# Moving the norms' small sums to VectorE, and giving the list scheduler a different clock, in an fp32 encoder kernel

## The chip, the cores and the metric

The kernel runs on one core of a Trainium2 chip, as one launch. The metric is the device time of that launch in microseconds. A core has a matrix engine (TensorE, PE in the profile, with its weight loads as PEld), VectorE (DVE), ScalarE (ACT), GpSimd (POOL) and SyncE (SP, which here only issues DMAs). Each engine works off its own instructions in the order in which they were written, and waits where an input isn't there.

## The reference

Two encoder layers on a sequence of 256 rows of 1024 numbers, in fp32. Each layer has a mixer and a feed-forward part:

```
h = rms_norm(x, n1);  proj = h @ w_in                # 1024 -> 2560
qa, ka, va, qd, kd, vd, qc, kc, vc = split(proj)     # heads of 64
q, k of each group: rms_norm per head, d and c with rotary positions
out_a = neighbourhood_attention(4 heads, bias rpb)   # 2-D window
out_d = dilated_window_attention(6 heads)            # 3 patterns merged
out_c = gqa_block_attention(6 heads, 2 kv heads)     # full
x = x + concat(rms_norm(out_a), rms_norm(out_d), rms_norm(out_c)) @ w_out
h = rms_norm(x, n2);  g, u = split(h @ w_gate_up)    # 2 x 2816
g = depthwise_conv(g, 3 taps) + b
x = x + (gelu(g) * u) @ w_down
```

## The kernel before

**Arithmetic.** Every matrix product is three matmuls on parts of 32-bit numbers: each factor is split into a high part (rounded by a copy) and a low part (the difference), and `mm3` adds high x high, high x low and low x high. Weights arrive by DMA as `wp_raw`; ACT casts `wp_hi`, DVE subtracts `wp_lo`. The same is done with activations: `act_hT` (the normed x, transposed), `act_ch` and `act_cl` (softmax results, transposed, and later the gated values), `act_mixT_hi` and `act_mixT_lo` (attention results). Results stand in PSUM tiles `psa_a` (512 columns) and `psw_w`.

**Stages of a layer.** x is transposed into hT; the projections are made in the order d0, d1, cq, akv, aqk; the three groups of heads follow in the order d, c, a. For a head: scores (half-height matmuls, `act_o` for d), softmax on DVE and ACT (`act_s2k`), transposes by a matmul with `const_ident`, then the weighing of values (`const_v`). The next projections, and then the out-projections of finished groups, are handed out between the heads, so that PE has work while the softmax runs. After the last out-projections x (`const_x`) is normed and transposed again and the feed-forward part begins.

**Norms of q and k.** `normed` squares a piece of the projection (for d0, d1 and cq on ACT with a running sum; for the others on ACT with a reduction on DVE: `small_ss`), calls `rstd_of` (`small_ms` = ss / 64 + eps, then `small_rstd` = ms to the power -1/2, always on POOL), and scales the piece into `act_z`. For d0 and d1 DVE scales the first half of the heads in one instruction and ACT the others one by one. `mean_squares` does the like for the norms of x (`small_ssx`, `small_s1x`, `small_mex`, `small_rx`); `small_he` is an eps derived from it. `group_rstd` sums squares of a finished attention group (`act_sqm`, added on POOL).

**Bias rows.** `na_repeat` copies 28 rows of 31 numbers 64 times beside each other on POOL (`act_nab` from `small_few`) and writes them to DRAM, from where `na_diagonals` reads them back skewed.

**Kept weights.** The last six out-projection units of the second layer are loaded and split during the first layer's feed-forward part, written to DRAM (`dram_khi`, `dram_klo`), and loaded again in the second layer's attention by DMAs that POOL issues (`wp_hi<-dram_khi` and so on; the last into tiles `act_kc` and `act_qc` of earlier stages).

**What sets the order.** The program is first recorded by `Plan`, 5,000-odd operations with their dependences. `Plan.order` is a list scheduler with a clock of its own: `cost` gives each operation a duration, `handover` the time from one engine's result to another's start, `LANDS` the assumed landing times of the first 13 DMAs, and two constants in `order` the start and landing of every later one. At each step it takes, over all engines, the operation that can start first; between equals the lower rank wins, which is the place in the program plus offsets, among them `PLACES`, a table from an operation's number to a shift. `emit` writes the instructions in that order, which is why nearly every row of the profile has one line, L496. Tiles come from pools of few buffers, and a load waits until its buffer's last reader is done.

Of the kernel before, what the change touches and what calls it, by code (L numbers as in the profile page):

```python
# [14 lines left out]
AF = mybir.ActivationFunctionType  # L15
# [3 lines left out]
P = 128  # L19
# [32 lines left out]
LANDS = (4100, 3300, 5300, 3450, 6000, 6900, 7700, 8800, 9700, 10600, 11500, 11550, 11600)  # L52
# [177 lines left out]
def handover(a, b):  # L230
    return HANDOVER.get((a, b), 52 if b == "PE" else 60)
# [321 lines left out]
def encoder_kernel(  # L553
# [400 lines left out]
    for l in range(DEPTH):  # L954
# [59 lines left out]
        me, rx = mean_squares(f"n1{l}")  # L1014

        he = small.tile([P, NT], F32, tag="he", name=f"he{l}", bufs=2)
        nc.gpsimd.tensor_scalar(he, me, EPS, None, ALU.mult)

        wv.until("d0")

# [619 lines left out]
```

## Time and profile before

| | us |
|---|---|
| three runs | 606.33, 606.69, 609.0 (median 606.69) |
| the profiled execution | 605.31 |
| its span | 603.5 |
| PE busy in it | 595.9 |
| DVE busy | 484.2 |
| ACT busy | 425.2 |
| POOL busy | 86.7 |

The span is the time from the first to the last instruction in the profile of one execution; the execution's own time is longer by what lies around it. The profile has views for the busy time of each engine, for groups of like instructions, for the waits of an engine (what ended its idle time), for the chain of work that ended last, and a timeline of single instructions.

### The profile page before, as it was taken

What the parts mean: (1) busy time and instruction counts of PE and PEld (TensorE: products, weight loads), DVE (VectorE), ACT (ScalarE), POOL (GpSimd) and SP (SyncE); (2) the same over time, 40 slices, a digit from 0 to 9 for tenths busy, and PEclk for the clock granted to TensorE, in tenths of its full rate; (3) what the DMA queues carried; (4) which work ended last, traced back from release to release, by engine and by line L of the source; (5) the groups of instructions that cost most, each with busy time, mean ns of one, the idle gap of its engine ahead of it and who ended that gap; (6) DMA issues with size and microseconds to landing.
All of it is one profiled execution on the core that took longest, in us unless ns stands there. A gap on an engine that the chain in (4) does not pass through costs nothing.

```text
span 603.5 us, 9483 instructions
## 1 busy us (share of the span) xinstructions
PE 595.9 (99%) x3304; PEld 505.3 (84%) x3304; DVE 484.2 (80%) x991; ACT 425.2 (70%) x1049; POOL 86.7 (14%) x130
## 2 busy tenths in 40 slices
PE   9999999999999999999999999999999999999997
PEld 6887888888888888888888787887888888888886
DVE  4799988989679898877968897858877777787766
ACT  7879899786666776656688897776765656556652
POOL 2761131105200000000021314412000000000000
PEclk9999999999999999999999999999999999999999
DMA  8992305355589899997655444932565556555501
GB/s 290 379 267 79 119 31 170 138 198 205 172 251 310 287 333 340 320 307 283 208 183 169 141 140 175 325 132 71 185 235 183 173 202 209 174 179 205 183 27 71
DMA packets 89503, 121.42 MB, mean 201 GB/s; under 512 B 10072, under 2 KB 72120, under 8 KB 89456
## 3 DMA queue, kind: packets, MB, share of 16 engines
q1 hardware_dynamic: 87184, 112.17, 55.6%
q0 software_dynamic: 1728, 8.39, 4.0%
q8 instruction: 26, 0.43, 0.3%
q10 hardware_dynamic: 544, 0.26, 0.1%
q14 instruction: 21, 0.17, 0.1%
HBM read 110.93 MB, written 9.88 MB: 200 GB/s over the span
## 4 chain that ended last, share of the span: by engine, by line
PE 77%; DVE 6%; POOL 5%; DMA 5%; issue 3%; ACT 3%; SPq 1%; DVEq 0%; POOLq 0%; ACTq 0%
PE psw_w L496 47%; PE psa_a L496 30%; POOL small_rstd L496 2%; ACT act_s2k L496 2%; DVE const_x L496 1%; DMA wp_hi<-dram_khi 1%; DMA wp_lo<-dram_klo 1%; SPq L496 1%; DVE wp_lo L496 1%; DVE act_z L496 1%; DMA const_x<-in_x_dram 1%; DMA small_few<-in_rpb_dram 1%; POOL small_ms L496 1%; DVE act_s2k L496 1%; ACT wp_hi L496 0%
## 5 line engine op out<-in xcount | busy, mean ns | idle before, releaser
L496 DVE TENSOR_TENSOR wp_lo<-wp_raw,wp_hi 128x512 fp32r<-128x512 f32 (+1 forms) x316 | 233.4, 767 | 43.6 <-ACT wp_hi L496 38.8
L496 ACT CAST wp_hi<-wp_raw 128x512 fp32r<-128x512 f32 (+1 forms) x316 | 201.7, 689 | 28.4 <-PE psw_w L496 21.2
L496 PE MATMUL psw_w<-act_hT,wp_hi 128*128 128x512 f32 x704 | 178.1, 393 | 0.4 <-DVE act_hT L496 0.4
L496 PEld LDWEIGHTS psw_w<-act_hT,wp_hi 128*128 128x128 f32 x704 | 128.6, 188 | 26.6 <-DVE act_hT L496 1.2
L496 PE MATMUL psa_a<-wp_hi,act_hT 128*128 128x512 f32 x320 | 104.1, 398 | 0.3 <-ACT act_hT L496 0.3
L496 PE MATMUL psw_w<-act_hT,wp_lo 128*128 128x256 f32 x704 | 96.4, 279 | 0.0
L496 PEld LDWEIGHTS psw_w<-act_hT,wp_lo 128*128 128x128 f32 x704 | 92.5, 188 | 4.2
L496 ACT COPY act_s2k<-psw_w 128x256 f32<-128x256 f32 x88 | 32.2, 372 | 57.0 <-PE psw_w L496 56.8
L496 PEld LDWEIGHTS psa_a<-wp_hi,act_hT 128*128 128x128 f32 x320 | 59.1, 188 | 12.3 <-ACT act_hT L496 0.5
L496 PE MATMUL psa_a<-wp_lo,act_ch 128*128 128x512 f32 (+1 forms) x176 | 67.8, 387 | 0.0
L496 PE MATMUL psa_a<-wp_hi,act_ch 128*128 128x512 f32 (+1 forms) x176 | 67.6, 388 | 0.0
L496 PE MATMUL psa_a<-wp_hi,act_cl 128*128 128x512 f32 (+1 forms) x176 | 64.8, 387 | 0.0
L496 PE MATMUL psa_a<-wp_lo,act_hT 128*128 128x512 f32 x160 | 62.8, 395 | 0.0
L496 DVE TENSOR_TENSOR act_s2k<-psw_w,act_s2k 128x256 f32<-128x256 f32 x88 | 36.5, 421 | 28.8 <-ACT act_s2k L496 28.5
L496 PEld LDWEIGHTS psa_a<-wp_hi,act_cl 128*128 128x128 f32 x176 | 33.0, 188 | 6.8
L496 PEld LDWEIGHTS psa_a<-wp_lo,act_ch 128*128 128x128 f32 x176 | 33.0, 188 | 6.8
L496 PEld LDWEIGHTS psa_a<-wp_hi,act_ch 128*128 128x128 f32 x176 | 32.9, 188 | 6.7
L496 DVE SCALAR_TENSOR_TENSOR act_s2k<-act_s2k,act_cw,act_s2k 128x255 f32<-128x255 f32 x88 | 36.8, 477 | 0.1
L496 PEld LDWEIGHTS psa_a<-wp_lo,act_hT 128*128 128x128 f32 x160 | 30.1, 188 | 6.1 <-DVE wp_lo L496 0.2
L496 POOL TENSOR_TENSOR small_rstd<-small_ms,const_mh 128x2 f32<-128x2 f32 (+3 forms) x26 | 32.3, 1242 | 14.1 <-DVE small_ms L496 12.5
L496 ACT ACTIVATE act_s2k<-act_s2k 128x512 f32<-128x512 f32 x22 | 13.9, 633 | 25.2 <-DVE act_s2k L496 25.2
L496 ACT ACTIVATE act_s2k<-act_s2k,small_rs 128x256 f32<-128x256 f32 x64 | 29.2, 511 | 0.8 <-DVE small_rs L496 0.7
(130 smaller groups left out, 800.1 us busy)
## 6 DMA issues: line engine op xcount, KB each, us to landing
wp_raw<-in_w_gate_up_dram SPq DMA_DIRECT2D x44, 1024.0 KB, 4.9
wp_raw<-in_w_down_dram SPq DMA_DIRECT2D x22, 1024.0 KB, 4.9
wp_raw<-in_w_in_dram SPq DMA_DIRECT2D x16, 512.0 KB, 5.6
wp_raw<-in_w_in_dram SPq DMA_DIRECT2D x8, 1024.0 KB, 6.6
wp_raw<-in_w_out_dram SPq DMA_DIRECT2D x8, 768.0 KB, 4.3
wp_raw<-in_w_in_dram SPq DMA_DIRECT2D x16, 256.0 KB, 3.6
dram_khi<-act_mixT_hi SPq DMA_DIRECT2D x4, 768.0 KB, 4.1
dram_klo<-act_mixT_lo SPq DMA_DIRECT2D x4, 768.0 KB, 10.0
```

What stands on the lines that cost most here:

```text
L496: getattr(o.engine.real, o.method)(*map(real, o.args), **{k: real(v) for k, v in o.kw.items()})
```

## The change

Four things, with no change to the mathematics and with the same matmuls:

1. `rstd_of` makes `small_ms` always on VectorE; `small_s1x`, `small_mex` and `small_he` go to VectorE too. The power stays on POOL. 30 small instructions move.
2. `na_repeat` copies in four instructions of 16 repetitions each.
3. `normed` lets one engine scale a whole piece: ACT the d1 pieces, head by head, DVE all others, d0 among them.
4. The scheduler's clock: earlier `LANDS`, 180 instead of 52 ns from any engine to PE, later start (POOL's DMAs) and landing (all DMAs) of transfers, and a new `PLACES` table.

```diff
-LANDS = (4100, 3300, 5300, 3450, 6000, 6900, 7700, 8800, 9700, 10600, 11500, 11550, 11600)
+LANDS = (4000, 3300, 4800, 3450, 5400, 6200, 7500, 7900, 8600, 9400, 9950, 10150, 10350)
...
 def handover(a, b):
-    return HANDOVER.get((a, b), 52 if b == "PE" else 60)
+    return HANDOVER.get((a, b), 180 if b == "PE" else 60)
 PLACES = {
-    69: 675, 174: 69, 175: 485, 176: 81, 201: 382, 299: 271, 372: 236, 390: 27, 400: 25, 409: 64, 508: 25, 568: 374,
...
+    51: 27, 63: -214, 81: 932, 98: 230, 130: -463, 139: 398, 155: 65, 169: 146, 175: 246, 176: 223, 183: -207,
...
                 ring = e if i < self.first_loads else "SP"
-                end = max(at + 1360, wires.get(ring, 0.0))
+                end = max(at + (2100 if e == "POOL" else 1360), wires.get(ring, 0.0))
...
-                end = wires[ring] + 1000
+                end = wires[ring] + 1600
                 if i < self.first_loads:
                     end = LANDS[sum(p.method == "dma_start" for p in ops[:i])]
...
         ms = small.tile([P, n], F32, tag="ms", name=f"ms_{name}")
-        by = nc.vector if width > HD else nc.gpsimd
-        by.tensor_scalar(ms, ss, 1.0 / width, eps, ALU.mult, ALU.add)
+        nc.vector.tensor_scalar(ms, ss, 1.0 / width, eps, ALU.mult, ALU.add)
...
-        nc.gpsimd.tensor_tensor(s1, ss[:, :, 0], ss[:, :, 1], op=ALU.add)
+        nc.vector.tensor_tensor(s1, ss[:, :, 0], ss[:, :, 1], op=ALU.add)
         me = small.tile([P, NT], F32, tag="mex", name=f"me_{name}", bufs=2)
-        nc.gpsimd.tensor_scalar(me, s1, 1.0 / D, EPS, ALU.mult, ALU.add)
+        nc.vector.tensor_scalar(me, s1, 1.0 / D, EPS, ALU.mult, ALU.add)
...
-        nc.gpsimd.tensor_copy(
-            rows_.rearrange("p (n c) -> p n c", c=RPB_C),
-            nabs["few"].unsqueeze(1).to_broadcast([NR, GRID_W, RPB_C]),
-        )
+        for i in range(0, GRID_W, 16):
+            nc.gpsimd.tensor_copy(
+                rows_.rearrange("p (n c) -> p n c", c=RPB_C)[:, i : i + 16],
+                nabs["few"].unsqueeze(1).to_broadcast([NR, 16, RPB_C]),
+            )
...
-        nc.gpsimd.tensor_scalar(he, me, EPS, None, ALU.mult)
+        nc.vector.tensor_scalar(he, me, EPS, None, ALU.mult)
...
-            n = nh // 2 if name[0] == "d" else nh
-            nc.vector.tensor_tensor(
-                z[:, :n],
-                ps[:, : n * HD].rearrange("p (h d) -> p h d", d=HD),
-                r[:, :n].unsqueeze(2).to_broadcast([P, n, HD]),
-                op=ALU.mult,
-            )
-            for h in range(n, nh):
-                nc.scalar.activation(z[:, h], ps[:, h * HD : (h + 1) * HD], AF.Copy, scale=r[:, h : h + 1])
+            if name[:2] == "d1":
+                for h in range(nh):
+                    nc.scalar.activation(z[:, h], ps[:, h * HD : (h + 1) * HD], AF.Copy, scale=r[:, h : h + 1])
+            else:
+                nc.vector.tensor_tensor(
+                    z[:, :nh],
+                    ps[:, :w].rearrange("p (h d) -> p h d", d=HD),
+                    r.unsqueeze(2).to_broadcast([P, nh, HD]),
+                    op=ALU.mult,
+                )
```

Since the scheduler's clock and table change, most instructions change places. Three of them follow; a tile's number at the end of its name is its buffer, and the numbers differ between the kernels.

**PE, first layer, ahead of the first softmax result.** `act_hT` with `wp_hi` or `wp_lo` is a projection matmul of 512 columns; the row with `const_ident` and `act_s2k` is the first transpose of a softmax result. Before, the rows from the last projection's start to it:

```order
L496 MATMUL psa_a_309<-wp_hi_142,act_hT_148 128x512
L496 MATMUL psa_a_309<-wp_lo_150,act_hT_148 128x512
L496 MATMUL psa_a_309<-wp_hi_142,act_hT_148 128x512 x2
L496 MATMUL psa_a_309<-wp_lo_150,act_hT_148 128x512
L496 MATMUL psa_a_309<-wp_hi_142,act_hT_148 128x512 x2
L496 MATMUL psa_a_309<-wp_lo_150,act_hT_148 128x512
L496 MATMUL psa_a_309<-wp_hi_142,act_hT_148 128x512 x2
L496 MATMUL psa_a_309<-wp_lo_150,act_hT_148 128x512
L496 MATMUL psa_a_309<-wp_hi_142,act_hT_148 128x512
L496 MATMUL psw_w_170<-const_ident_89,act_s2k_220 128x128
```

These are all the rows between the last scores and that transpose: 12 matmuls. After, the last rows ahead of it:

```order
L499 MATMUL psa_a_298<-wp_lo_146,act_hT_143 128x512
L499 MATMUL psa_a_292<-wp_hi_242,act_hT_143 128x512
L499 MATMUL psa_a_292<-wp_lo_251,act_hT_143 128x512
L499 MATMUL psa_a_292<-wp_hi_242,act_hT_143 128x512
L499 MATMUL psa_a_298<-wp_hi_137,act_hT_143 128x512 x2
L499 MATMUL psa_a_298<-wp_lo_146,act_hT_143 128x512
L499 MATMUL psa_a_298<-wp_hi_137,act_hT_143 128x512
L499 MATMUL psa_a_298<-wp_hi_242,act_hT_143 128x512
L499 MATMUL psa_a_298<-wp_lo_251,act_hT_143 128x512
L499 MATMUL psw_w_116<-const_ident_88,act_s2k_205 128x128 x4
```

There are 24 matmuls between the last scores and that transpose now (the ten shown and 14 ahead of them), and five more stand ahead of the scores.

**PE, first layer, from the second half of the out-projections to the feed-forward part.** `const_ident` with `const_x` transposes x, `act_hT` with `wp_hi` first in such a row is the feed-forward part. Before:

```order
L496 MATMUL psw_w_124<-const_ident_89,const_x_79 128x128
L496 MATMUL psw_w_83<-const_ident_89,const_x_79 128x128
L496 MATMUL psw_w_124<-const_ident_89,const_x_79 128x128 x3
L496 MATMUL psa_a_342<-wp_hi_142,act_mixT_lo_871 128x512
L496 MATMUL psw_w_83<-const_ident_89,const_x_79 128x128 x3
L496 MATMUL psa_a_160<-wp_hi_142,act_mixT_lo_871 128x512
L496 MATMUL psa_a_160<-wp_hi_142,act_mixT_hi_797 128x512
L496 MATMUL psa_a_160<-wp_lo_150,act_mixT_hi_797 128x512
L496 MATMUL psa_a_160<-wp_hi_142,act_mixT_lo_871 128x512
L496 MATMUL psw_w_117<-act_hT_148,wp_hi_244 128x512
```

After:

```order
L499 MATMUL psw_w_116<-const_ident_88,const_x_79 128x128
L499 MATMUL psw_w_123<-const_ident_88,const_x_79 128x128
L499 MATMUL psa_a_292<-wp_lo_146,act_mixT_hi_851 128x512
L499 MATMUL psa_a_292<-wp_hi_137,act_mixT_lo_862 128x512
L499 MATMUL psw_w_116<-const_ident_88,const_x_79 128x128 x3
L499 MATMUL psw_w_123<-const_ident_88,const_x_79 128x128 x3
L499 MATMUL psw_w_169<-act_hT_143,wp_hi_137 128x512
```

Of the five out-projection matmuls behind the first transposes of x two are left.

**POOL, second layer, the kept weights.** A DMA row loads a kept weight. Before:

```order
L496 TENSOR_TENSOR small_rstd_338<-small_ms_329,const_mh_85 128x2
L496 TENSOR_TENSOR act_sqm_918<-act_sqm_918,act_sqm_817 128x256
L496 DMA wp_hi_142<-dram_khi_2023 128x1536
L496 DMA wp_lo_255<-dram_klo_2053 128x1536
L496 TENSOR_SCALAR small_ms_356<-small_ss_410,small_he_3058 128x8
```

and the second load of `wp_hi_142`, further on:

```order
L496 TENSOR_TENSOR small_rstd_484<-small_ms_477,const_mh_85 128x2
L496 DMA act_kc_908<-dram_klo_2641 128x1024
L496 DMA act_kc_903<-dram_khi_2627 128x1024
L496 DMA act_qc_679<-dram_khi_2757 128x1024
L496 DMA wp_hi_142<-dram_khi_2340 128x1536
```

After:

```order
L499 TENSOR_TENSOR small_rstd_324<-small_ms_321,const_mh_83 128x2
L499 DMA wp_hi_137<-dram_khi_2028 128x1536
L499 DMA wp_lo_146<-dram_klo_2097 128x1536
L499 TENSOR_TENSOR act_sqm_917<-act_sqm_917,act_sqm_856 128x256
L499 DMA wp_lo_251<-dram_klo_2215 128x1536
```

and

```order
L499 TENSOR_TENSOR small_rstd_490<-small_ms_469,const_mh_83 128x2
L499 DMA act_kc_900<-dram_klo_2650 128x1024
L499 DMA wp_hi_137<-dram_khi_2345 128x1536
L499 DMA act_qc_709<-dram_khi_2738 128x1024
L499 DMA act_qc_720<-dram_klo_2763 128x1024
```

The first two loads have moved ahead of the sum of squares that they stood behind, and the second load of that `wp_hi` now stands behind one of the loads into `act_kc` and `act_qc` where it stood behind three.

33 rows, old and new, of the table PLACES are left out of this document.

## The prediction

> **What bounds the kernel now.** I read the page first: span, busy shares and chain.
>
> ```profile
> span 603.5 us, 9483 instructions
> PE 595.9 (99%) x3304; PEld 505.3 (84%) x3304; DVE 484.2 (80%) x991; ACT 425.2 (70%) x1049; POOL 86.7 (14%) x130
> PE 77%; DVE 6%; POOL 5%; DMA 5%; issue 3%; ACT 3%; SPq 1%; DVEq 0%; POOLq 0%; ACTq 0%
> ```
>
> TensorE (PE) carries the program: it is drawn busy for 99% of the span and holds 77% of the chain that ended last. The other 23% are places where the chain leaves it. The 99% flatters, because ends of matmuls are modelled; the pace is seen where the chain holds nothing else:
>
> ```profile
> 550.01 5.45 PE psa_a L496 x24
> 555.46 11.13 PE psw_w L496 x64
> ```
>
> 24 matmuls of 512 columns take 5.45 us, 227 ns each. The other row holds 32 of 512 and 32 of 256: (11.13 - 32 x 0.227) / 32 = 0.12 us for 256 columns. The change issues the same matmuls, so it can only remove what comes above this pace. Where that lies, the busy time by stretch tells (us of PE, PEld, DVE, ACT, POOL, then granted clock, DMA share, GB/s):
>
> ```profile
> 30.00:60.00 30.00, 29.55 (x163) 23.85 (x162) 28.39 (x84) 26.19 (x95) 11.86 (x20) 1.00 0.62 176
> 90.00:120.00 30.00, 29.81 (x188) 24.79 (x188) 27.09 (x66) 25.44 (x70) 4.43 (x5) 1.00 0.45 156
> 120.00:330.00 210.00, 210.00 (x1108) 180.24 (x1107) 173.50 (x305) 144.81 (x314) 19.09 (x29) 1.00 0.76 255
> 330.00:360.00 30.00, 29.93 (x177) 24.59 (x176) 27.17 (x90) 27.37 (x98) 8.38 (x12) 1.00 0.46 150
> 360.00:390.00 30.00, 29.23 (x192) 24.71 (x191) 23.57 (x56) 23.42 (x68) 12.16 (x18) 1.00 0.65 221
> 390.00:420.00 30.00, 28.90 (x182) 23.95 (x181) 22.38 (x57) 21.49 (x59) 6.88 (x10) 1.00 0.37 132
> ```
>
> The clock is full everywhere, and the first feed-forward part (120 to 330) shows no idle PE. PE waits only in the two attention parts, 30 to 120 and 330 to 420, where VectorE (DVE) is busy for 27 to 28 of 30 us. The timeline of PE gives the waits one by one (start, duration drawn, idle ahead and what ended it):
>
> ```profile
> 10.56 0.50 PE L496 MATMUL psa_a<-wp_hi,act_hT 128*128 128x512 f32 x1 [0.31 <-ACT act_hT L496]
> ...
> 47.25 0.39 PE L496 MATMUL psa_a<-wp_hi,act_hT 128*128 128x512 f32 x1
> 47.86 0.33 PE L496 MATMUL psw_w<-const_ident,act_s2k 128*128 128x128 f32 x1 [0.22 <-ACT act_s2k L496]
> ...
> 52.95 0.36 PE L496 MATMUL psw_w<-act_ch,const_v 128*128 128x256 f32 x1
> 53.43 0.39 PE L496 MATMUL psw_w<-act_cl,const_v 128*128 128x256 f32 x1
> ...
> 118.23 0.40 PE L496 MATMUL psa_a<-wp_hi,act_mixT_lo 128*128 128x512 f32 x1
> 118.82 0.50 PE L496 MATMUL psw_w<-act_hT,wp_hi 128*128 128x512 f32 x1 [0.19 <-DVE act_hT L496]
> ...
> 372.95 0.40 PE L496 MATMUL psa_a<-wp_hi,act_mixT_hi 128*128 128x512 f32 x1
> 374.11 0.50 PE L496 MATMUL psa_a<-wp_lo,act_mixT_hi 128*128 128x512 f32 x1 [0.77 <-DMA wp_lo<-dram_klo]
> ...
> 393.43 0.28 PE L496 MATMUL psw_w<-act_cl,const_v 128*128 128x256 f32 x1
> 394.31 0.50 PE L496 MATMUL psa_a<-wp_hi,act_mixT_hi 128*128 128x512 f32 x1 [0.60 <-DMA wp_hi<-dram_khi]
> ```
>
> A wait costs start to start less the pace. 47.25 to 47.86: 0.61 - 0.23 = 0.38. 52.95 to 53.43: 0.48 - 0.12 = 0.36. 118.23 to 118.82: 0.36. 372.95 to 374.11: 0.93. 393.43 to 394.31: 0.76. At 10.56 it is the 0.31 shown and about the 0.16 that the modelled ends hide elsewhere (0.38 - 0.22, 0.93 - 0.77). Sum 3.3 us. The idle PE of the windows quoted is 0.45 + 0.19 + 0.07 + 0.77 + 1.10 = 2.6 us, of which these rows' brackets after 30 us show 0.22 + 0.19 + 0.77 + 0.60 = 1.8. The rest, 0.8 us, is short waits with the hidden part that each brings (some 0.16 us); I estimate 2 us in all. So some 5.3 us of 603.5 are to be had.
>
> **The change, part by part.** The prices, as groups by form (count, busy us, mean ns of one, idle before, releaser):
>
> ```profile
> L496 POOL TENSOR_SCALAR small_ms<-small_ss,small_he 128x8 f32<-128x8 f32 x8 | 3.5, 438 | 23.4 <-DVE small_ss L496 13.9 <-ACT act_s2k L496 9.1
> L496 POOL TENSOR_TENSOR small_s1x<-small_ssx 128x2 f32<-128x2 f32 x4 | 1.4, 358 | 174.2 <-ACT act_s2k L496 174.2
> L496 DVE TENSOR_SCALAR small_ms<-small_ss 128x2 f32<-128x2 f32 x6 | 1.0, 164 | 0.1
> L496 DVE TENSOR_TENSOR act_z<-psa_a,small_rstd 128x512 f32<-128x512 f32 x4 | 2.7, 684 | 0.0
> L496 DVE TENSOR_TENSOR act_z<-psa_a,small_rstd 128x256 f32<-128x256 f32 x4 | 1.7, 425 | 4.5 <-ACT act_z L496 2.0 <-POOL small_rstd L496 1.7 <-issue 0.7
> L496 DVE TENSOR_TENSOR act_z<-psa_a,small_rstd 128x128 f32<-128x128 f32 x8 | 2.3, 289 | 1.7 <-POOL small_rstd L496 1.5 <-ACT act_z L496 0.2
> L496 ACT ACTIVATE act_z<-psa_a,small_rstd 128x64 f32<-128x64 f32 x24 | 5.9, 335 | 6.7 <-DVE act_z L496 4.6 <-POOL small_rstd L496 2.1
> L496 ACT ACTIVATE act_s2k<-psa_a 128x64 f32<-128x64 f32 x72 | 15.4, 255 | 2.3 <-PE psa_a L496 2.3
> ```
>
> Small sums: 30 operations leave GpSimd (POOL) for VectorE. One costs 0.44 us on POOL (128x8) and 0.164 us on DVE. DVE gets at most 30 x 0.164 = 4.9 us; the six ms that DVE does already show 0.1 us idle before them, so they cost no wait there. Each norm's chain, square, sum, power, scaling, gets about 0.27 us shorter. That pays only where the scaling is waited for: DVE's 1.7 + 1.5 us and ACT's 2.1 us idle behind small_rstd. None of it ends a PE wait quoted above directly, so the sum takes nothing for it, with 0 and +0.5 us as bounds.
>
> Scaling by one engine: per d0 piece (4 in all) DVE does 128x512 for 128x256 (+0.26 us) and ACT four 128x64 less; per d1 piece (4) DVE loses a 128x128 (-0.29) and ACT gets two 128x64. DVE: 4 x 0.26 - 4 x 0.29 = -0.1 us; ACT: 4 x (2 - 4) x 0.335 = -2.7 us. ACT is not full in the windows, so it is worth nothing by itself; bounds 0 and +0.3, since two idles of one half behind the other (2.0 and 4.6 us in the rows) end.
>
> Bias rows in four copies:
>
> ```profile
> 17.11 1.89 DVE L496 TENSOR_TENSOR wp_lo<-wp_raw,wp_hi 128x512 fp32r<-128x512 f32 x3
> 20.21 1.03 DVE L496 TENSOR_TENSOR wp_lo<-wp_raw,wp_hi 128x512 fp32r<-128x512 f32 x1 [1.21 <-ACT wp_hi L496]
> ...
> 18.71 1.99 POOL L496 COPY act_nab<-small_few 28x1984 f32<-28x1984 f32 x1 [2.98 <-DMA small_few<-in_rpb_dram]
> ```
>
> The copy keeps POOL for 1.99 us ahead of the first norm's sum. In the new order two quarters stand ahead of the first power, so the first norm gains about 1 us; PE has no wait between 10.56 and 47.25, so this too is cover, not time: 0. Four starts instead of one cost POOL a few tenths where it has idle time. The rows also show a subtraction of 1.03 us, begun while the copy ran, against 1.89 / 3 = 0.63 before.
>
> The Trainium skill, SBUF — State Buffer, section Who interferes with whom, says that a VectorE instruction with two SBUF inputs and a GpSimd instruction that reads SBUF exclude each other for a whole instruction. The 0.40 us of stretch agree. By it the quarters would hold DVE for at most 0.5 us at a time, and the gain of at most 0.4 us a layer would fall where PE doesn't wait: the sum stays.
>
> Planner's clock and places: this moves nearly everything, and here the time is made. Place by place, in the new order:
>
> - Start, wait of 0.47 at 10.56 for ACT's part of hT. Casts of weights stand in other places, and DVE's hT is waited for earlier. I take +0.3 (bounds -0.2 and +0.47).
> - First heads of the first layer. Ahead of the first transpose of a softmax result stand 17 more 512-wide matmuls (12 of them between scores and transpose: 24, not 12), 3.9 us of PE work, against some 0.7 us more on ACT. The 0.38 at 47.86 should go. Ahead of the first weighing of values PE has 3.9 us more too, but DVE four more wp_lo (4 x 0.63) and nine small sums (9 x 0.07 to 9 x 0.164, by the spacing below): 3.1 to 4.0 us. So of the 0.36 at 53.43, and of about 0.3 of short waits ahead of it, I take half to go. Together +0.85 (bounds 0 and +1.0).
> - End of the first attention. Between the last value matmul and the feed-forward part stand three matmuls less, between the last transposes of the first half of x and that part two instead of five. The chain that PE waits for there is no shorter. -0.7 = 3 x 0.23 on top of the 0.36 (bounds -0.7 and 0).
> - Reloads of kept weights in the second layer, next.
>
> ```profile
> 113.75 0.16 DVE L496 TENSOR_SCALAR small_ms<-small_ss 128x2 f32<-128x2 f32 x1
> 113.82 1.28 DVE L496 TENSOR_TENSOR wp_lo<-wp_raw,wp_hi 128x512 fp32r<-128x512 f32 x2
> ...
> 363.69 1.10 POOL L496 TENSOR_TENSOR act_sqm<-act_sqm,act_sqm 128x256 f32<-128x256 f32 x1 [4.97 <-ACT act_sqm L496]
> 364.74 0.80 POOL L496 DMA_DIRECT2D wp_hi<-dram_khi  x1
> ...
> 385.28 0.56 POOL L496 DMA_DIRECT2D wp_hi<-dram_khi  x1
> ...
> 365.52 8.54 DMA wp_lo<-dram_klo
> ...
> 385.28 8.98 DMA wp_hi<-dram_khi
> ```
>
> (The first two rows give the spacing of a small sum on DVE: 0.07 us.) The first reload stands in POOL's queue behind a sum that waited 4.97 us for ACT; the load of wp_lo then takes 8.54 us, and PE waits 0.93 for it. In the new order both loads come ahead of that sum and are held by their buffer alone; by my count of the matmuls between the buffer's last use and the need they have about 10 us of PE's work for 9.3 us of issue and transfer. The wait of 0.93 goes, barely. The load at 385.28 was issued behind three others of about its own 0.56 us and now stands behind one: 1.1 us earlier, against 0.76 of wait. I take +1.6 of 1.69; bounds 0 (the transfers share the queue differently) and +1.69.
>
> For this size, 768 KB, the Trainium skill (DMA: Bandwidth & Descriptors, section Anatomy of one DMA — SWDGE (gpsimd) path) gives 2.0 us plus bytes / 436e3, an estimate of 3.8 us. By it no reload would be waited for, and the 1.6 us would not be there to win; the trace has 8.54 and 8.98 and decides.
>
> - The short waits, 2 us by the estimate above: the new clock assumes 180 ns, not 52, from an engine's result to PE, which puts results further ahead wherever another matmul can be taken. I take 1.0 (bounds 0 and 2.0).
> - DVE's load: +4.9 - 0.1 us in parts of the program where it has 1.6 to 2.9 us idle per 30. I take -0.25 (bounds -3 and 0).
>
> Sum: 0.3 + 0.85 - 0.7 + 1.6 + 1.0 - 0.25 = 2.8 us gained. Against the profiled execution of 605.31 us that is 602.5. The median of the runs, 606.69, lies 1.38 above that execution, so the forecast is 603.9.
>
> **The rivals.**
> *All waits go.* The slack of 180 ns removes the waits named and the short ones, and none comes in their place: -5.3 us, 601.4. For it: the feed-forward part, planned by the same code, has none. Against it: the end of the first attention has less cover than before.
> *Given back.* VectorE is the bound of the attention parts: of its 4.9 us about half (2.3) comes back on PE, in front of transposes and value matmuls: -2.8 + 2.3 = -0.5, 606.2. For it: 28.39 and 27.17 of 30 us busy; against it: the spacing of 0.07, with which 30 sums are 2.1 us.
> *Slower.* A small sum waits in VectorE's queue for ACT's squares, as POOL did (9.1 us idle behind ACT for the 128x8 alone), and the wp_lo and softmax work behind it waits too. Twelve sums (d0, d1 and cq pieces, six a layer) depend on ACT's squares. If each stands one us too early, DVE loses 6 us a layer, of which its idle time in 30 to 60 and 330 to 360 hides 1.61 and 2.83: 7.6 us later, less 2.8 gained: 611.5. It decides from about 0.6 us each (2.0 + 0.8 = 2.8). Against it: POOL is off PE's path and its idle time tells nothing of the order on DVE, where the planner places a sum by its own estimate of the squares' end (row of 255 ns each).
> *Doesn't do what it says.* LANDS and start moves change only the first 12 us; the reloads' waits stay. It gains 0.3 to 1 us: 606.
>
> **How the numbers follow.** A change of 0.5%, 3.03 us (0.005 x 606.69), is about what a measurement here tells from none; that bound, 603.66, lies next to my forecast. Forecast 0.45, own range 602 to 605.4, of which 0.19 falls beyond the bound and 0.26 within. All waits go 0.22 (faster). Given back 0.17 and does nothing 0.05 (same). Slower 0.11. So faster 0.41, same 0.48, slower 0.11. The range runs from 600.6 (601.4 less 0.8, the rest of short waits if my estimate of 2 is low) to 607.3 (given back, and the end of the first attention one us worse); outside it lie slower, 0.11, and some 0.07 below.
>
> **What would show it.** Right: no idle marked DMA on PE around 372 and 393, none at 47 and 53 us; a wait of about 1 us for hT, not 0.36, where the first feed-forward part begins; DVE some 3 to 5 us busier, ACT 2.7 us and POOL about 10 us less; the same number of matmuls. Wrong: idle of DVE ahead of small_ms released by ACT; a reload landing over 10 us after its issue; PE idle for act_cl or act_hT in new places in 30 to 120 us. If the time is the same although those waits are gone, the end of the attention parts took it back.

## The result, and the profile after

The changed kernel takes 602.26 us (median of 4 runs, 602.02 to 602.48), the kernel before 607.07 us beside it (4 runs, 606.33 to 609.0). The ratio is 0.9916 with a 95% interval of 0.9892 to 0.994: 4.8 us less. Measured again later it was 602.78 against 607.93 us, ratio 0.991 (0.9887 to 0.9934). The forecast of 603.9 us lay 1.6 us too high, and the time fell within its range; of the cases, it lies between the forecast and "all waits go" (601.4), nearer to the latter. The profiled execution took 602.47 us, 2.84 less than that of before; where the other 2 us come from is part of what follows.

Part of it is TensorE's granted clock, which the profiler gives for each run: of the 51 runs of the kernel before that stand beside the experiments, the 27 with a mean granted clock of 0.999 or 1.000 took 605.1 to 608.4 us (median 606.7) and the 24 with 0.994 to 0.998 took 607.9 to 611.4 (median 609.1), while all of the changed kernel's ten runs had 0.999 or 1.000 (median 602.5); at the full clock the change is worth some 4.3 us.

The page of the changed kernel, busy shares and chain:

```profile
span 600.7 us, 9486 instructions
PE 594.5 (99%) x3304; PEld 506.0 (84%) x3304; DVE 487.8 (81%) x1017; ACT 424.2 (71%) x1041; POOL 74.7 (12%) x106
PE 95%; DVE 2%; ACT 1%; DMA 1%; issue 1%; POOL 0%; SPq 0%; POOLq 0%
```

The busy shares hardly tell a difference. The chain does: PE holds 95% of it where it held 77%, and GpSimd and the reloads have left it. The same stretches as before:

```profile
30.00:60.00 30.00, 30.00 (x166) 24.86 (x165) 28.98 (x86) 27.33 (x105) 9.18 (x15) 1.00 0.66 206
90.00:120.00 30.00, 28.86 (x181) 23.89 (x180) 27.30 (x67) 25.83 (x71) 4.20 (x5) 1.00 0.47 160
330.00:360.00 30.00, 30.00 (x173) 24.54 (x171) 25.36 (x85) 26.55 (x91) 5.10 (x5) 1.00 0.33 107
360.00:390.00 30.00, 30.00 (x215) 25.68 (x215) 24.73 (x63) 24.02 (x70) 12.20 (x16) 1.00 0.71 239
390.00:420.00 30.00, 30.00 (x187) 26.09 (x184) 23.83 (x62) 22.79 (x63) 5.23 (x7) 1.00 0.51 180
```

In both attention parts PE is drawn busy throughout, but for 90 to 120, where it is idle for 1.14 us against 0.19 before. The view of PE's waits (us in total, times, longest) names what is left:

```profile
PE psw_w L499 <- DVE act_hT L499: 1.1, 1, 1.1
PE psw_w L499 <- POOL const_mh L499: 1.0, 1, 1.0
PE psa_a L499 <- ACT act_hT L499: 0.3, 1, 0.3
```

The second is the start of the program, which both kernels have. The first is the wait ahead of the first feed-forward part; the third, at 7.57 us, is for ScalarE's part of hT, as the wait at 10.56 was before. In PE's timeline the waits at 47 and 53 us are gone. At the first reload two matmuls stand at the pace, where there was a wait of 0.93 us, and at the feed-forward part there is a gap:

```profile
373.08 0.40 PE L499 MATMUL psa_a<-wp_hi,act_mixT_hi 128*128 128x512 f32 x1
373.31 0.40 PE L499 MATMUL psa_a<-wp_lo,act_mixT_hi 128*128 128x512 f32 x1
...
117.00 0.82 PE L499 MATMUL psw_w<-const_ident,const_x 128*128 128x128 f32 x6
118.87 0.50 PE L499 MATMUL psw_w<-act_hT,wp_hi 128*128 128x512 f32 x1 [1.06 <-DVE act_hT L499]
```

I summed for each stretch what PE's matmuls take above the pace (start to start, less 0.2275, 0.1177 or 0.109 us by width, half for the half-height ones), for all profiled executions:

| us above the pace | 0-8 | 8-20 | 20-40 | 40-60 | 90-130 | 330-350 | 350-400 | 400-420 | all but 0-8 |
|---|---|---|---|---|---|---|---|---|---|
| before | 1.60 | 0.98 | 0.01 | 1.77 | 1.75 | 0.96 | 4.45 | 1.00 | 14.09 |
| after | 2.98 | 0.29 | 0.01 | 0.55 | 2.60 | 0.36 | 2.57 | 0.20 | 9.86 |
| after, again | 3.37 | 0.42 | 0.01 | 0.52 | 2.55 | 0.44 | 2.35 | 0.38 | 10.05 |

The first 8 us are mostly a matter of luck. ScalarE's first cast there waits for the first weights, and their DMA, issued at 1.6 us in both kernels, landed at 5.22 us in the one profile and at 6.14 in the other. Before, then after, in ScalarE's timeline:

```profile
5.24 0.62 ACT L496 CAST wp_hi<-wp_raw 128x512 fp32r<-128x512 f32 x1 [2.21 <-DMA wp_raw<-in_w_in_dram]
```

```profile
6.16 0.62 ACT L499 CAST wp_hi<-wp_raw 128x512 fp32r<-128x512 f32 x1 [3.16 <-DMA wp_raw<-in_w_in_dram]
```

Over the 14 profiled executions of this study the excess of this stretch runs from 1.60 to 3.60 us, and the 1.60 is the kernel before's. It follows that landing (5.22 to 6.88 us): the excess up to 20 us is the landing less 2.64 to 2.68 us in the three profiles with the order of before, and less 2.79 to 2.91 in seven of the eight with the new order and its table (2.46 in the eighth, `after_ht2` below, where PE waits 0.6 us for the load of x). So for the same landing the new order wins only about 0.2 us up to 20 us; most of the 0.69 in the column 8-20 is the wait at 10.56 that now stands at 7.57. Behind 20 us the two profiles differ by 13.11 - 9.56 = 3.55 us. Together that is some 3.75 us, against 4.3 between the runs at the full clock and 4.8 between all.

### The profile page after: what moved, and what is told of

Read it like the earlier page. It is cut to its first block, busy times and chain, and to the rows that moved or that the text cites. A ratio compares the mean times of both kernels' runs of the same rounds, so it can differ in the third digit from the quotient of the medians.

```text
span 600.7 us, 9486 instructions
## 1 busy us (share of the span) xinstructions
PE 594.5 (99%) x3304; PEld 506.0 (84%) x3304; DVE 487.8 (81%) x1017; ACT 424.2 (71%) x1041; POOL 74.7 (12%) x106
## 4 chain that ended last, share of the span: by engine, by line
PE 95%; DVE 2%; ACT 1%; DMA 1%; issue 1%; POOL 0%; SPq 0%; POOLq 0%
PE psw_w L499 51%; PE psa_a L499 44%; DVE const_x L499 1%; DMA wp_raw<-in_w_in_dram 1%; DVE wp_lo L499 1%; ACT act_s2k L499 0%; DVE act_cl L499 0%; DVE act_mixT_lo L499 0%; ACT act_ch L499 0%; ACT act_hT L499 0%; SPq L499 0%; DVE act_hT L499 0%; POOL act_sqm L499 0%; POOL small_rstd L499 0%; ACT act_mixT_hi L499 0%
## 5 line engine op out<-in xcount | busy, mean ns | idle before, releaser
L499 PE MATMUL psa_a<-wp_hi,act_hT 128*128 128x512 f32 x320 | 102.3, 396 | 0.3 <-ACT act_hT L499 0.3
L499 ACT ACTIVATE act_s2k<-act_s2k,act_cw 128x256 f32<-128x256 f32 x44 | 24.1, 595 | 14.1 <-DVE act_s2k L499 14.1
```

The source lines that it names most:

```text
L499: getattr(o.engine.real, o.method)(*map(real, o.args), **{k: real(v) for k, v in o.kw.items()})
```

## The experiments

**Order and operations apart.** An operation can be recorded for one engine, placed by the scheduler, and at the end written out in another form in the same place. So two kernels could be made that cross the change: the new order with the old operations, and the old order with the new ones.

```diff
+            nc.instead[i] = [(nc.gpsimd, "tensor_scalar", (ms, ss, 1.0 / width, eps, ALU.mult, ALU.add), {})]
 # in emit, at the place of operation i:
-                getattr(o.engine.real, o.method)(...)
+                for engine, method, args, kw in self.instead.get(i, [(o.engine, o.method, o.args, o.kw)]):
+                    getattr(engine.real, method)(...)
```

(The same for s1x, mex, he, the copies and the scaling; the reverse in the kernel before.)

> The changed kernel's order to the last instruction, but with the operations of before in their places: the 30 small sums on GpSimd, the bias rows in one copy, d0 and d1 pieces scaled by two engines. Theory (the order made the time, the operations are cover): 602.3 us as the changed kernel, within 1 us, and no new wait of TensorE; GpSimd about 11 us busier, VectorE 3.5 us less busy. Rival (the shorter norm chains made the time): 604.5 us or more, with TensorE waiting around 47 and 330 to 350 us.

> The order of before, but with the new operations in the places of the old: sums on VectorE, four short copies where the long one stood, one engine for a piece. Theory (the order made the time): within 1 us of before, with the waits for the two reloads (0.94 and 0.76 us) still there. Rival (the shorter norm chains made the time): 2.5 us or more faster than before. A third possibility, sums standing too early in VectorE's queue since the order was not made for them: 1 to 3 us slower.

| | old operations | new operations |
|---|---|---|
| old order | 608.22 us (in four sets of runs the median lay between 607.05 and 608.22) | 608.12 us, ratio to before 1.0012 (0.9992 to 1.0033) |
| new order | 605.08 us, 0.9954 (0.9937 to 0.9971) | 602.26 us, 0.9916 (0.9892 to 0.994) |

All 12 runs of the new order with the old operations had the full granted clock, 16 of the 29 of the kernel before beside them, and 8 of the 12 of the old order with the new operations. Among the runs with the full clock the medians are 605.1, 606.8 and 607.6 us.

In the old order the new operations give nothing, as the theory had it. The reloads' waits are still there in its PE timeline, and longer:

```profile
376.35 0.50 PE L503 MATMUL psa_a<-wp_lo,act_mixT_hi 128*128 128x512 f32 x1 [1.46 <-DMA wp_lo<-dram_klo]
396.85 0.51 PE L503 MATMUL psa_a<-wp_hi,act_mixT_hi 128*128 128x512 f32 x1 [0.90 <-DMA wp_hi<-dram_khi]
```

But the new order with the old operations brings only 3.1 of the 4.8 us, and 1.7 of 4.3 at the full clock. Here the rival was right: in this order the operations are worth 2 us or more (605.08 against 602.26 and 602.78). Its excess has 1.00 us in 20 to 40 and 1.08 in 40 to 60, where the changed kernel has 0.01 and 0.55.

**Which operation.** Two kernels with the new order and one old operation each, beside the changed kernel on the same chip.

```diff
 # new_sums_gpsimd: the 30 sums only
+        nc.elsewhere(nc.gpsimd)          # emitted on GpSimd, in its place
 # new_scale_old: the scaling only
+            half = [(nc.vector, "tensor_tensor", (z[:, :n], ps[:, : n * HD], r[:, :n]), {"op": ALU.mult})]
+            # d0: half, then n activations on ScalarE; d1: half in place of the first n activations
```

> The changed kernel once more, as the base for the others of this call. Theory: the ratio to the kernel before is 0.9916 as measured, and its runs lie within 0.5 us of each other where those of the kernel before spread over 4 to 5 us (605.1 to 609.9 in the last call), since no reload is waited for any more. Rival (the first measurement was a lucky chip): ratio 0.995 or more, the same spread.

> The changed kernel in the same order, with only the 30 small sums back on GpSimd in their places. With all three operations undone in the new order it took 605.08 us, against 602 to 603.5 for the new ones; in that trace ScalarE's four scalings of a half piece stand ahead of weight casts and wait for the power (25.41 us). Theory A (the scaling on ScalarE does it, by holding up casts behind it): within 0.5 us of the changed kernel. Theory B (the slower sums do it): 1.5 us slower or more.

> The changed kernel in the same order, with only the scaling as before: VectorE one half and ScalarE the other half of d0 and d1 pieces. Theory A (ScalarE's scalings hold up the casts behind them): 1 to 2 us slower than the changed kernel, with TensorE waiting for wp_hi around 27 and 41 us. Theory B (the sums do it): within 0.5 us of it.

The changed kernel took 602.78 us (602.07 to 603.18), the sums on GpSimd 603.45 (602.45 to 603.75, ratio to before 0.9921, 0.9898 to 0.9945), the old scaling 604.12 (603.68 to 604.78, 0.9935, 0.9911 to 0.9959). The runs of the changed kernel spread over 1.1 us, those of the kernel before over 5.6 (605.8 to 611.38). All runs of the three had the full granted clock. So the scaling is worth about 1.3 us here, and the sums about 0.7, which lies between theory A's bound and B's and whose runs overlap with the changed kernel's. The excess agrees: with the old scaling 0.85 us in 20 to 40 and 0.94 in 330 to 350, 1.4 more than after in the two; with the old sums 0.58 in 20 to 40. The four short copies were not tried alone. ScalarE's timeline with the old scaling shows one way in which it costs time:

```profile
23.41 0.93 ACT L506 ACTIVATE act_z<-psa_a,small_rstd 128x64 f32<-128x64 f32 x4 [0.42 <-DVE act_z L506]
24.20 1.16 ACT L506 CAST wp_hi<-wp_raw 128x512 fp32r<-128x512 f32 x2
```

Four scalings stand ahead of two weight casts, wait 0.42 us for VectorE's half and take 0.8: the casts come that much later than they would without them, for which the order was made. That is not all of it: of the 0.85 us, 0.41 stand ahead of matmuls that waited for weights (at 25.62 and 38.75 us) and 0.30 ahead of a transpose that waited for a scaled piece (34.69). Each is so short that PE's waits don't list wp_hi, which the expectation had at 27 and 41 us. In the kernel with all three undone a matmul waits for a late cast. So it does with the sums alone on GpSimd, where ScalarE's scalings wait for the power behind the slower sum, and the casts behind the scalings; ScalarE, then PE:

```profile
37.26 1.91 ACT L506 ACTIVATE act_z<-psa_a,small_rstd 128x64 f32<-128x64 f32 x8 [0.47 <-POOL small_rstd L506]
39.03 2.19 ACT L506 CAST wp_hi<-wp_raw 128x512 fp32r<-128x512 f32 x4
...
39.72 0.96 PE L506 MATMUL psa_a<-wp_hi,act_hT 128*128 128x512 f32 x3 [0.29 <-ACT wp_hi L506]
```

**The reloads alone.** In the kernel before five instructions of GpSimd's queue change places.

```diff
-sqm, hi59, lo59, ... kc10, kc00, qc00, hi61
+hi59, lo59, sqm, ... hi61, kc10, kc00, qc00
```

> The kernel before with five reloads moved in GpSimd's queue and nothing else: the first two kept weights ahead of the sum of squares that they stood behind (364.74 us), and the third unit's high part ahead of the three loads into act_kc and act_qc that it stood behind (385.28). Theory (the order of GpSimd's queue costs the two waits): the loads are then held by their buffers alone, whose last readers end at 363.7 and 384.6 us; 0.85 and 0.65 us earlier, so 1.5 us faster than before, with 0.1 us of each wait left. Rival (the transfers share the queues and land when they land): no change, both waits of 0.94 and 0.76 us stay.

It took 606.26 us (605.64 to 609.17), ratio 0.998 (0.9962 to 0.9999): some 1 to 2 us, with an interval that just leaves out no change. But 11 of these 12 runs had the full granted clock against 16 of 29 of the kernel before, and among those the difference is 606.23 to 606.78, 0.55 us of the expected 1.5. The rest is that the clock fell in 1 run of 12 and not in 13 of 29, a gain of the moved reloads too if such waits are what lowers it. In its profile, the slowest of its runs (609.17) and the one whose clock was 0.997, both waits are gone from their places, and two others stand at the next pair of loads:

```profile
400.70 0.73 PE L503 MATMUL psa_a<-wp_hi,act_mixT_hi 128*128 128x512 f32 x2 [0.88 <-DMA wp_hi<-dram_khi]
402.51 0.68 PE L503 MATMUL psa_a<-wp_lo,act_mixT_hi 128*128 128x512 f32 x1 [0.96 <-DMA wp_lo<-dram_klo]
```

The windows there (length, then PE's busy time; the granted clock is third from the end):

```profile
400.00:402.60 2.60, 0.95 (x4) 0.58 (x4) 0.65 (x2) 1.58 (x5) 0.72 (x1) 1.00 0.07 25
402.60:406.00 3.40, 3.40 (x11) 2.72 (x12) 0.48 (x1) 1.15 (x3) 0.00 (x0) 0.51 0.00 0
```

Right behind the two waits the granted clock fell to half for 3.41 us, and matmuls of 512 columns followed each other every 0.43 us where the pace is 0.23. So the two waits cost PE their own 1.84 us and about 1.4 us of slow matmuls behind them.

**The reloads late again.** The reverse in the changed kernel:

```diff
-hi59, lo59, sqm
+sqm, hi59, lo59
```

> The changed kernel with its first two reloads of kept weights put back behind the sum of squares in GpSimd's queue, nothing else. They are issued about 366.1 and 366.9 us instead of 362.0 and 362.8; with 8.5 to 9.1 us of transfer the second lands at 375.4 to 376.0, and TensorE needs it at 373.3. Theory (a reload's landing hangs on its issue, and its scatter is what spread the runs of before): 2.1 to 2.7 us slower than the changed kernel, with the wait at that place, and the runs spread over 2 us or more. Rival (transfers land when the queues let them): under 1 us slower.

The theory fell. The time is that of the changed kernel, 602.43 us (602.06 to 603.86), ratio 0.9915 (0.9889 to 0.9941), though in the profile the loads were issued 4.2 us later and PE used them at the same place. GpSimd's and SyncE's issues, and PE at the place of use:

```profile
366.23 0.79 POOL L506 DMA_DIRECT2D wp_hi<-dram_khi  x1
367.01 0.54 POOL L506 DMA_DIRECT2D wp_lo<-dram_klo  x1
...
367.93 0.37 SPq L506 DMA_DIRECT2D wp_raw<-in_w_down_dram  x1
...
373.23 0.40 PE L506 MATMUL psa_a<-wp_hi,act_mixT_hi 128*128 128x512 f32 x1
373.46 0.43 PE L506 MATMUL psa_a<-wp_lo,act_mixT_hi 128*128 128x512 f32 x1
```

The second load took 6.34 us to land (at 373.35, a tenth of a microsecond before its use at 373.46), not 8.5. The same two queues before, and the time to landing that the view of one tile gives for SyncE's 1 MB load:

```profile
365.40 0.37 SPq L496 DMA_DIRECT2D wp_raw<-in_w_down_dram  x1
364.74 0.80 POOL L496 DMA_DIRECT2D wp_hi<-dram_khi  x1
365.52 0.55 POOL L496 DMA_DIRECT2D wp_lo<-dram_klo  x1
...
L496 SPq DMA_DIRECT2D wp_raw<-in_w_down_dram x1: 367/367/367, 365.4 to 365.4; - x1
DMA to landing us min/median/max: 8.9/8.9/8.9
```

and after:

```profile
367.78 0.37 SPq L499 DMA_DIRECT2D wp_raw<-in_w_down_dram  x1
361.98 0.78 POOL L499 DMA_DIRECT2D wp_hi<-dram_khi  x1 [2.72 <-ACT act_z L499]
362.76 0.54 POOL L499 DMA_DIRECT2D wp_lo<-dram_klo  x1
...
L499 SPq DMA_DIRECT2D wp_raw<-in_w_down_dram x1: 368/368/368, 367.8 to 367.8; - x1
DMA to landing us min/median/max: 4.8/4.8/4.8
```

Before, the 1 MB load of `w_down` was issued 0.12 us ahead of the second reload, and both took long: 8.9 and 8.54 us. After, it comes 5.0 us behind the reload: 4.8 and 6.14 us. In the late kernel it comes 0.9 us behind it: 8.1 for the big load, 6.34 for the reload. So with 0.12 us between the issues both were slow, and with 0.9 us the first kept its short time and the second paid. The other profiles agree. In the old order with the new operations the two were again issued 0.12 us apart: 9.06 us for the big load, 9.10 for the reload. With the reloads moved in the kernel before the big load came 1.07 us behind: 8.09 and 7.22. In the seven profiles where it came 5 us behind it took 4.7 to 5.0 and the reload 6.1 to 7.5, so the 6.14 and 6.34 are at the short end, and the margin of a tenth in the late kernel had some luck in it. That reading puts the wait of before down to the other queue's load next to the reload; GpSimd's own order would count only by putting the two side by side, and the moved reloads changed that distance as well as the place. That a load of SyncE was moved in before alone, to show it from that side, was not tried.

**The end of the first attention.** Two attempts to win back the wait of 1.2 us in the changed kernel.

```diff
 # after_ht
-PE: x t0, mm, mm, x t1 x3        ACT: square, hT          DVE: const_x, hT
+PE: x t0, x t1 x3, mm, mm        ACT: hT, square          DVE: hT, const_x
 # after_ht2: PE as above
-ACT: cast, hT a0, hT b0, hT b1, hT a1     DVE: wp_lo, const_x, hT a0, const_x, hT a1, hT b0
+ACT: hT a0, hT a1, hT b0, hT b1, cast     DVE: const_x, hT a0, hT a1, const_x, hT b0, hT b1, wp_lo
```

> The changed kernel with five instructions moved at the end of the first layer's attention: three transposes of x ahead of two out-projection matmuls, ScalarE's first part of hT ahead of a square, VectorE's first part of hT ahead of an update of x. Theory (the wait of 1.2 us ahead of the feed-forward part is this chain, which has lost three matmuls of cover): the first part of hT is ready 0.6 to 0.7 us earlier, 601.6 us against 602.3. Rival (what was moved back is late next: the update of x, and the transposes behind it): no change, the wait moves to the second half of hT some 1 us later.

> The changed kernel with the end of the first attention in another order: as in the last try the transposes of x ahead of two matmuls, and further on ScalarE both parts of hT of the first transposed tile ahead of the second tile's and of a cast, on VectorE one update of x ahead of hT, both parts of hT ahead of the other update, and one weight subtraction behind all of them. In the last try the feed-forward part began 0.6 us earlier, and 1.2 us were lost again behind it, where the next transposes waited for the tile that hT's second part was still read from. Theory (that tile's reader was the cause): 0.6 to 0.8 us faster than the changed kernel. Rival (VectorE's work in this stretch is the bound, whatever its order): the same time.

The first: 603.51 us (603.1 to 604.72), ratio 0.9932 (0.9907 to 0.9958). The rival's result: the wait ahead of the feed-forward part fell from 1.06 to 0.28 us, and the next transposes of x waited 1.24:

```profile
118.99 0.50 PE L506 MATMUL psw_w<-act_hT,wp_hi 128*128 128x512 f32 x1 [0.28 <-DVE act_hT L506]
119.33 0.29 PE L506 MATMUL psw_w<-act_hT,wp_lo 128*128 128x256 f32 x1
119.46 0.40 PE L506 MATMUL psw_w<-act_hT,wp_hi 128*128 128x512 f32 x1
119.69 0.28 PE L506 MATMUL psw_w<-act_hT,wp_lo 128*128 128x256 f32 x1
121.22 0.55 PE L506 MATMUL psw_w<-const_ident,const_x 128*128 128x128 f32 x3 [1.24 <-DVE act_hT L506]
```

The second: 603.33 us (602.68 to 603.85), ratio 0.9922 (0.9896 to 0.9948). The 1.24 is gone, and smaller waits have come behind it; the excess in 90 to 130 is 2.74 us against 2.60 and 2.55. Again the rival. The busy time of this stretch, before and in the changed kernel, gives a reason:

```profile
113.00:121.00 8.00, 7.81 (x43) 6.03 (x42) 8.00 (x17) 6.18 (x15) 1.08 (x1) 1.00 0.71 261
113.00:121.00 8.00, 6.86 (x37) 5.23 (x36) 8.00 (x17) 6.72 (x18) 1.08 (x1) 1.00 0.73 260
```

VectorE is drawn busy for 8.00 of 8.00 us in both; the changed kernel has six matmuls less there to cover it. By that VectorE, not TensorE, is the bound here, which fits two orders of its work that moved the wait and didn't end it. A kernel with less work on VectorE there was not tried.

**The scheduler's clock without the table.** Three kernels with the new operations and `PLACES = {}`.

```diff
-PLACES = { 51: 27, 63: -214, ... }
+PLACES = {}
 # no_table_52, and no_table_old_clock with LANDS, 1360 and 1000 as before too:
-    return HANDOVER.get((a, b), 180 if b == "PE" else 60)
+    return HANDOVER.get((a, b), 52 if b == "PE" else 60)
```

> The changed kernel with an empty PLACES table: its operations, its new clock, no hand-set shifts. Theory (the clock's slack of 180 ns is most of it, the table the rest): faster than the same without the new clock (the third of these kernels) by 2 us or more, slower than the changed kernel by 2 to 5 us. Rival (the table is most of it): 6 us or more slower than the changed kernel.

> As the kernel with the empty table and the new clock, but with 52 instead of 180 ns from an engine to TensorE. Theory (the slack towards TensorE is the part of the clock that counts): as slow as the one with the old clock altogether, within 0.7 us, with more short waits of TensorE in 30 to 120 and 330 to 420 us. Rival (the later start and landing of transfers count): as fast as the one with the new clock, with the waits for reloads gone.

> The changed kernel's operations with an empty table and the clock of before (LANDS, 52 ns, start and landing of transfers). Theory: the slowest of the three without a table, 2 us or more behind the one with the new clock; waits for reloads as in the kernel before. Rival: the clock makes no difference without a table made for it.

618.22, 617.87 and 618.05 us; ratios to before 1.0186 (1.015 to 1.0221), 1.0169 (1.0143 to 1.0195) and 1.0162 (1.013 to 1.0194). The scheduler's clock alone makes no difference that these runs can tell, and without a table 16 us are lost: both rivals. The first two rows of PE's waits with the new clock, then with the old:

```profile
PE psw_w L479 <- ACT act_ch L479: 4.1, 3, 1.7
PE psw_w L479 <- DVE act_hT L479: 3.2, 2, 1.9
```

```profile
PE psw_w L479 <- ACT act_ch L479: 4.2, 3, 2.2
PE psw_w L479 <- DVE act_hT L479: 3.5, 2, 2.0
```

Long single waits of 1.7 to 2.2 us decide there, which 130 ns of slack don't touch. Part of the loss is again TensorE's granted clock: 17 of the 18 runs have means of 0.987 to 0.997, and the one at 1.000 took 614.21 us, 3.5 to 4.9 less than the other five of its kernel. What the new clock is worth together with a table can't be read from these runs, since each table was made for one clock.

## Why the prediction was right, step by step

The prediction put the gain in waits of the two attention parts, and it came from there. By the excess in the two profiles:

- **Start**: forecast +0.3. Measured, about 0.2 for the same landing of the first weights. The 0.69 us less in 8 to 20 is mostly the wait at 10.56 that has moved to 7.57; the other 0.9 of the 1.4 us more in the first 8 is the later landing (6.14 against 5.22).
- **First heads**: forecast +0.85, measured 1.22 in 40 to 60. Both waits went whole, not one and a half, although VectorE is busy for 28.98 of 30 us there, against 28.39 before.
- **End of the first attention**: forecast -0.7, measured -0.85. The count of matmuls taken away (3 x 0.23) was a good measure; VectorE, busy for all 8 us of the stretch, had no time to make up for it.
- **Reloads**: forecast +1.6, measured 1.9 in 350 to 400. The size was right, and a step behind it was wrong: "in the new order both loads come ahead of that sum" was taken as the cause, with 9.3 us for issue and transfer. With the sum put back ahead the wait did not return. By the times to landing the 8.54 us held a collision with a load of another queue that was issued 0.12 us earlier; with that load 0.9 us or more behind it the transfer took 6.1 to 7.5. The fit that the Trainium skill gives in DMA: Bandwidth & Descriptors, section Anatomy of one DMA — SWDGE (gpsimd) path, 3.8 us as an estimate for this size, was not reached in any of them.
- **Short waits**: forecast +1.0, measured about 1.4 (0.60 in 330 to 350, 0.80 in 400 to 420). That the slack of 180 ns brings this, as the prediction gave for a reason, was not shown: without a table it changes nothing that the runs can tell.
- **The operations as cover, 0**: this step failed as to the size. They are worth nothing in the old order, 2 to 3 us in the new. The prediction named work that hides them (no PE wait between 10.56 and 47.25) and looked for waits that exist in the profile of before. It didn't ask what stands behind a scaling in ScalarE's queue: weight casts, which an order made for the shorter queue puts closer to their use. The quarter copies were also dearer than the "few tenths" of the prediction: 0.59 to 1.60 us each, 8.0 us in all against 4.3 for the two long ones, in idle time of GpSimd. And ScalarE got only 1.0 us less busy (424.2 after 425.2), not 2.7; one of its scalings now takes 0.392 us on average, not 0.335.
- **VectorE's load**: forecast -0.25, seen none outside the end of the attention. The load itself was undersized. For 20 of the 30 sums, with two operands from memory, one takes 0.22 us, not the 0.164 of the row it was priced from. All 30 take 6.0 us where 4.9 was the most forecast; VectorE's busy time, in which overlapping instructions count once, rose by 3.6 (487.8 after 484.2):

```profile
L499 DVE TENSOR_SCALAR small_ms<-small_ss,small_he 128x8 f32<-128x8 f32 x8 | 1.8, 224 | 3.1 <-ACT act_s2k L499 3.1
L499 DVE TENSOR_SCALAR small_ms<-small_ss 128x2 f32<-128x2 f32 x6 | 1.0, 162 | 0.0
```

The first row also shows the slower rival at work on a small scale, and one of the prediction's signs of being wrong: VectorE idles 3.1 us behind ScalarE's squares over 8 sums, 0.4 each. The prediction had it decide from 0.6, over 12 sums. None of the waits that PE's view lists goes back to it.

The terms add up to 0.2 + 1.2 - 0.85 + 1.9 + 1.4 = 3.85 us, against the 2.8 forecast, 4.3 measured at the full clock and 4.8 over all runs. The 1.05 us between the forecast and this sum come from the short waits (0.4), the first heads (0.35), the reloads (0.3) and VectorE's load (0.25), less 0.25 for the start and the end of the attention. The first heads and the reloads lie beyond the prediction's own upper bounds of 1.0 and 1.69. So the places were right and the sizes only roughly; the operations' share and TensorE's granted clock were not in the sum.

Why the runs of the kernel before spread over up to 5.6 us and those of the changed one over 1.1 at most is in part on record: each run's mean granted clock is, and it parts the runs of before into two groups 2.4 us apart. Apart from the start and the end, five drops of the clock stand in the profiles: one with the moved reloads and four without a table. Each is to half for 3.41 us, which lowers a run's mean by 0.003 (0.5 x 3.41 / 605), so a mean of 0.997 is about one drop and 0.994 two. Ahead of each PE had been idle for 1.7 to 2.0 us of the last 3.4; no profile of the changed kernel has more than 1.2 us of such idle time, and none has a drop.

What stays open: that the waits cause the drops is read from their order in time and was not tested, and five stretches of 1.7 to 2.3 us of idle time in the kernels without a table passed without one. The one profile of the kernel before has the full clock, so which of its waits grows long enough in the slower runs isn't shown. The profiles of before, of the old order with new operations and of the moved reloads have 4.45, 5.46 and 3.79 us above the pace in 350 to 400, the last another 3.86 in 400 to 420; the changed kernel has 2.35 to 2.57 in its two profiles. That fits reloads that land late in some runs. Some 0.5 us between the 3.75 of the two profiles and the 4.3 of the runs at the full clock have no place either.

## What to carry to other kernels

A long DMA wait is first a question of what else was issued next to it: before moving a late load in its own queue, look at the other queues in the microsecond around its issue, and compare its time to landing with that of the same load elsewhere in the trace. Look at each run's granted clock before medians are compared: a wait of TensorE can cost more than its own length. An operation that is hidden today has a price in an order that is made without it; cost it by what stands behind it in its engine's queue, not only by the waits that the profile shows. And compare profiles stretch by stretch against the engine's pace, with the stretches that scatter set apart, before two single executions are subtracted.

## What was not expected of the hardware

The landing of the very first weight load, issued at 1.6 us in all 14 profiles, lay between 5.2 and 6.9 us, which moved the first 8 us by 2.0 us (1.60 to 3.60 us above the pace). Two loads of 0.75 and 1 MB from two queues cost each other by how far apart they were issued: at 0.12 us both were slow in two executions (8.5 and 9.1 us for the reload, 8.9 and 9.1 for the big load); at 0.9 and 1.1 us the first took 6.3 and 7.2, as with the other 5 us away (6.1 to 7.5), and the second 8.1 instead of 4.7 to 5.0. Behind two waits of PE, 1.84 us together, its granted clock was half for 3.41 us, and matmuls of 512 columns came 0.43 us apart instead of 0.23. A VectorE sum with a second operand from memory took 0.222 to 0.224 us for 4 to 8 columns and 0.220 for 2, against 0.162 with a constant (2 columns): the operand costs 60 ns, the columns next to nothing.
